# Six raw weight places and twelve input slots in the input stage of a hybrid S5 / forgetting-attention block

## The chip, the cores and the metric

One Trainium2 chip, one core. The metric is the device time of one execution in microseconds (us), the median of several runs. Engines are called PE (TensorE, matmuls and transposes), DVE (VectorE), ACT (ScalarE), POOL (GpSimd) and SP (SyncE, which here issues most transfers). Each engine runs its own instructions in order and waits on semaphores for the others.

## The reference, cut to what matters

```python
u = rms_norm(h, norm_mix)                       # x: (1, 1024, 1024) float32
proj = u @ w_in                                 # u_ssm (512), q, k, v (512 each), f (8), gates (2048)
y_ssm = gelu(s5_ssm(u_ssm, lam, dt, b, c, d))   # 32 groups, 64 complex states each, scan over 1024 tokens
glu_a, glu_b = split(y_ssm @ w_glu);  out_a = glu_a * sigmoid(glu_b)
out_b = forgetting_attention(q, k, v, f + b_forget) @ w_fox_o
h = h + (sigmoid(g_a) * out_a + sigmoid(g_b) * out_b) @ w_mix_out
m = rms_norm(mem, norm_mem_kv);  k, v = split(m @ w_mem_kv)   # 256 memory tokens, 4 heads of 128
h = h + cross_attention(rms_norm(h), k, v)
h = h + (silu(f_a) * f_b) @ w_ffn_out           # f_a, f_b = rms_norm(h) @ w_ffn_in
out = rms_norm(h)
```

Everything is float32. The change concerns the first stage (norms of `mem` and `x`, keys and values of the memory, `u_ssm`) and one step of the state-space stage.

## The kernel before, in words

**Arithmetic.** A float32 product is made of three matmuls. `split` writes a high part on ACT (a cast) and the rest on DVE, or on POOL where asked (a subtraction); `mm3` multiplies high by high, high by low and low by high.

**Stages.** `stage_in`, `stage_ssm` (32 gate products, with the state-space work of four quarters `q` among them), the attention, and a tail with mixing, cross-attention and the feed-forward part. The input stage keeps its tiles in a pool `xin`, closed before `stage_ssm` opens its own pool `qp` in the same memory.

**The input stage.** `ORDER_IN` is a list of steps written out by hand. `stage_in` walks through it and calls the function of each step's letter:

- `F` loads a tile of 128 tokens (`m`, `n` of `mem`, 0 to 7 of `x`) into an input slot; `G` loads a gain, spread over all partitions, into such a slot as well. There are 8 slots (tag `xt`).
- `Q` squares and sums on ACT, `R` makes the reciprocal root (`rsqrt`), `S` scales the tile by root and gain (`g`: on ACT and POOL), `T` transposes half a tile on PE, `E` evacuates and splits it into `mT` or `uT`.
- `D` loads a raw weight of 512 KB (0 to 3 keys, 4 to 7 values, 8 to b the state-space input from `w_in`) into a raw place, tag `raw`, of which there are 2; `W` splits it (`g`: low part on POOL). The split frees the place. The same two places serve the gate weights of the next stage.
- `K`, `V`, `U` are the products for keys, values and `u_ssm` (`U21`: quarter 2, second half of the tokens); `k`, `v`, `u` evacuate them. `k3` and `v` also store keys and values to memory. The tiles `us` that `u` fills reuse the four places of keys and values (tag `kv`), so they wait for these stores.
- `L0` issues the loads of the state-space parameters, `L1` transposes them on PE, `P` runs the next piece of their preparation on DVE.
- `X` runs warm-up matmuls on a constant at the start.

The order of emission is a priority: a scheduler at compile time merges the steps on each engine by its own estimate of what is ready, so the instructions of neighbouring steps interleave. What is once in an engine's order, or in SP's, then waits in that order.

**Roots.** `rsqrt` has two forms. With `pool`, POOL raises to the power -0.5 and DVE adds one Newton step (three instructions). Without, DVE makes a first guess from the bits and three Newton steps (ten instructions). Before, `mem` uses the first, `x` the second.

**State-space weights.** `S5.weights(q)` computes three tables for a quarter: `fb` (POOL, with scratch `w1`, `w2`), `Gm` (products of decay powers with `c` into the same scratch on POOL, subtracted on DVE), and `EC`, `ES` by doubling (POOL, the last two doublings on DVE). `turn_weights(q)` and `states(q)` use them on PE between gates 4 + 7q and 5 + 7q; `states` first loads `xg`, which `u` has stored.

Of the kernel before, what the change touches and what calls it, by code (L numbers as in the profile page):

```python
# [9 lines left out]
F32 = mybir.dt.float32  # L10
# [4 lines left out]
ALU = mybir.AluOpType  # L15
# [4 lines left out]
P = 128  # L20
D = 1024
# [17 lines left out]
RSLOT_LATE = (0, 1, 2, 3, 4, 4, 5, 5, 6, 6, 7, 7)  # L39

ORDER_IN = """
G0 Fm Qm Fn D1 X24 Qn Rm D0 Sm F1 G1 Tm0 Rn Em0 Sn Tn0 F0 Tm1 W0 Q0 Tn1 En0 F2 Q1 W1g En1 Em1 K0 D2 F3 K1 R0
S0 T00 T01 k0 E00 Q2 W2g D3 E01 D4 S1 T10 Q3 W3 k1 D5 K3 K2 W4 E10 W5 D6 R1 k2 T11 k3 S2 F4 Q4 V0 F5 S3g T30
E11 D7 Q5 F7 T20 R2 T21 E21 E20 S4 E30 W6 W7 T40 V1 D8 S5 E40 W8 T31 V2 L0 T41 E31 V3 D9 Db T50 F6 Q6 v T51 W9
E51 U00 Da Q7 L1 E41 u00 R3 S6 Wa T60 E50 S7 T61 T70 Wbg E61 U10 E60 P0 U20 u10 T71 E70 E71 u20 P1 U21 U11 U30
P2 u30 U31 u11 u31 U01 u21 P3 P4 P5 u01
"""

# [18 lines left out]
def f32(ap):  # L67
    return ap.bitcast(F32)
# [50 lines left out]
class Block:  # L119
    BANKS = {"mm": 3, "sc": 2, "pv": 2, "misc": 1}  # L120

    def __init__(self, ctx, tc):
        self.tc, self.nc = tc, tc.nc
        nc = self.nc
        self.V, self.A, self.G, self.T, self.S = nc.vector, nc.scalar, nc.gpsimd, nc.tensor, nc.sync
        self.const = ctx.enter_context(tc.tile_pool(name="const", bufs=1))
        self.small = ctx.enter_context(tc.tile_pool(name="small", bufs=3))
        self.wpool = ctx.enter_context(tc.tile_pool(name="wpool", bufs=4))
        self.dram = ctx.enter_context(tc.tile_pool(name="dram", bufs=1, space=DRAM))
        self.psum = ctx.enter_context(tc.tile_pool(name="psum", bufs=2, space=PSUM))  # L130
        self.ident = self.const.tile([P, P], F32, name="ident")
        make_identity(nc, self.ident)
        self.mhalf = self.const.tile([P, 1], F32, name="mhalf")
        nc.vector.memset(self.mhalf, -0.5)
        self.junk = self.const.tile([P, 512], BF16, name="junk")
        self.nbank = 0
# [197 lines left out]
def stage_in(B, xp, s5, x, mem, g_mix, g_kv, w_in, w_mem_kv, uT, u_d, kv_d):  # L334

    V, A, T, S, small = B.V, B.A, B.T, B.S, B.small  # L340
    junk = xp.tile([P, D], BF16, name="junk")
    mT = Act(xp, "mT", 4, 8, ML, kg=4, name="m")
    tiles, gain, ss, rs, raw, w, ps, us, kv = {}, {}, {}, {}, {}, {}, {}, [], []
    names = {"m": -2, "n": -1, **{str(t): t for t in range(NT)}}

    def xtile(name="xt"):
        return xp.tile([P, D], F32, tag="xt", bufs=8, name=name)

    def fetch(t):
        tiles[t] = xtile()  # L350
        S.dma_start(tiles[t], mem[(t + 2) * P:(t + 3) * P, :] if t < 0 else x[t * P:(t + 1) * P, :])

    def gains(i):
        gain[i] = xtile("gain")
        S.dma_start(gain[i], (g_kv if i == 0 else g_mix).partition_broadcast(P))

    def square(t):
        if t % 2 == 0:
            ss[t // 2] = small.tile([P, 2], F32, name="ss2")
        A.activation(junk, tiles[t], AF.Square, scale=1.0 / 32, accum_out=ss[t // 2][:, t % 2:t % 2 + 1])  # L360

    def root(i):
        rs[i] = B.rsqrt(ss[-1][:, i % 2:i % 2 + 1] if i < 0 else ss[i], pool=i < 0)

    def scale(t, pool):
        i = t // 2
        r = rs[t][:, 0:1] if t < 0 else rs[i][:, t % 2:t % 2 + 1]
        B.norm_scale(tiles[t], tiles[t], r, gain[0 if t < 0 else 1], pool=pool)

    def turn(t, b):  # L370
        ps[t, b] = B.turn(tiles[t], b, ("misc", "pv")[b])

    def evac(t, b):
        B.turned(ps.pop((t, b)), b, *((mT, t + 2) if t < 0 else (uT, t)))

    def wget(i):
        if i < 4:
            src = w_mem_kv[:, i * P:(i + 1) * P]
        elif i < 8:
            src = w_mem_kv[2 * (i - 4) * P:2 * (i - 3) * P, 512:1024]  # L380
        else:
            src = w_in[:, C_U + (i - 8) * P:C_U + (i - 7) * P]
        raw[i] = B.wpool.tile([P, RAW], F32, tag="raw", bufs=2, name="raw")[:, :D]
        S.dma_start(raw[i].rearrange("p (k c) -> p k c", k=D // src.shape[-1]),
                    src.rearrange("(k p) c -> p k c", p=P))

    def wsplit(i, pool):
        hl = [B.wpool.tile([P, WSLOT], F32R, tag=t_, name=t_)[:, :D] for t_ in ("whi", "wlo")]
        if i < 8:
            B.split(*hl, raw.pop(i), pool)  # L390
        else:

            B.split(*[t_.rearrange("p (k n g) -> p k n g", k=8, n=16) for t_ in hl],
                    raw.pop(i).rearrange("p (k g n) -> p k n g", k=8, g=8), pool)
        w[i] = [t_.rearrange("p (k c) -> p k c", k=2 if 4 <= i < 8 else 8) for t_ in hl]

    def keys(h):
        ps["k", h] = B.bank("mm")
        B.gemm_t(ps["k", h][:, :ML], *w[h], mT, 0, 8)

    def keys_out(h):
        if not kv:
            kv.extend(xp.tile([P, D], F32R, tag="kv", bufs=4, name="kv") for _ in range(4))
        cs = slice(h * ML, (h + 1) * ML)
        B.split(kv[0][:, cs], kv[1][:, cs], ps.pop(("k", h))[:, :ML])
        if h == 3:
            for i in range(2):
                S.dma_start(kv_d[i], f32(kv[i]))

    def values(kk):  # L410
        wh, wl = w[4 + kk]
        for t in range(2):
            if kk == 0:
                ps["v", t] = B.bank("sc")
            for k in (2 * kk, 2 * kk + 1):
                B.mm3(ps["v", t], *mT.tok(k, t), wh[:, k % 2, :], wl[:, k % 2, :], k == 0, k == 7)

    def values_out():
        for t in range(2):
            cs = slice(t * 512, (t + 1) * 512)  # L420
            B.split(kv[2][:, cs], kv[3][:, cs], ps.pop(("v", t)))
        for i in range(2, 4):
            S.dma_start(kv_d[i], f32(kv[i]))

    def ssm_in(q, h):
        ps["u", q, h] = B.bank("mm")
        B.gemm_t(ps["u", q, h], *w[8 + q], uT, h, 8)

    def ssm_out(q, h):
        if h == 0:  # L430
            us.append(xp.tile([P, D], F32, tag="kv", bufs=4, name="us"))
        uv = us[q].rearrange("p (t c) -> p t c", t=8)
        A.copy(uv[:, :, 64 * h:64 * h + 64], ps.pop(("u", q, h)).rearrange("p (c t) -> p t c", t=8))
        if h == 1:
            S.dma_start(u_d[q].rearrange("t p c -> p t c"), uv)

    prep = s5.prepare()

    acts = {"F": lambda a: fetch(names[a]), "G": lambda a: gains(int(a)), "Q": lambda a: square(names[a]),
            "R": lambda a: root(names[a]),  # L440
            "S": lambda a: scale(names[a[0]], a[1:] == "g"),
            "T": lambda a: turn(names[a[0]], int(a[1])), "E": lambda a: evac(names[a[0]], int(a[1])),
            "D": lambda a: wget(int(a, 16)), "W": lambda a: wsplit(int(a[0], 16), a[1:] == "g"),
            "K": lambda a: keys(int(a)), "k": lambda a: keys_out(int(a)), "V": lambda a: values(int(a)),
            "v": lambda a: values_out(), "U": lambda a: ssm_in(int(a[0]), int(a[1])),
            "u": lambda a: ssm_out(int(a[0]), int(a[1])), "L": lambda a: s5.load(int(a)),
            "P": lambda a: next(prep, None), "X": lambda a: B.warm(int(a))}
    for step in ORDER_IN.split():
        acts[step[0]](step[1:])
# [661 lines left out]
class S5:  # L1111
# [149 lines left out]
    def weights(self, q):  # L1261
# [5 lines left out]
        def bpow(tab, n):  # L1267
            return tab[:, :n, j4].rearrange("p k j -> p j k").unsqueeze(3).to_broadcast([P, 4, n, 16])

        def bvec(v, n):  # L1270
            return v[:, j4, :].unsqueeze(2).to_broadcast([P, 4, n, 16])
# [15 lines left out]
        Gp = Gm.rearrange("p (j two t m) -> p j two t m", two=2, t=8, m=16)  # L1287
        gv = [w.rearrange("p (j t m) -> p j t m", j=4, t=8) for w in (w1, w2)]
        for o in range(2):
            G.tensor_tensor(out=gv[0], in0=bpow(self.la[0], 8), in1=bvec(self.cT[o], 8), op=ALU.mult)  # L1290
            G.tensor_tensor(out=gv[1], in0=bpow(self.la[1], 8), in1=bvec(self.cT[1 - o], 8), op=ALU.mult)
            for two in range(2):
                h = slice(64 * two, 64 * two + 64)
                dst = Gp[64 * o:64 * o + 64, :, two]
                if o == 0:
                    V.tensor_sub(dst, gv[0][h], gv[1][h])
                else:
                    V.scalar_tensor_tensor(out=dst, in0=gv[0][h], scalar=-1.0, in1=gv[1][h],
                                           op0=ALU.mult, op1=ALU.subtract)
# [511 lines left out]
```

## Time and profile before

| | |
|---|---|
| runs | 1593.13, 1590.36, 1592.80 us; median 1592.8 |
| span of the profiled execution | 1586.7 us; the profile gives no device time of its own for it |
| what lies around the span, taken from the median | 6.1 us |
| mean granted TensorE clock | 0.988 |
| busy | PE 1534.0, DVE 1019.5, ACT 655.2, POOL 254.3 us |

The profile is one execution. A line of a timeline reads: start, length, engine, source line, operation, output<-inputs, shapes, count, and in brackets the idle time of the engine before it and what released it. In the chain of waits each line is a piece of the chain that ended last. The granted clock is a share of full speed. The lines shown in the prediction are not repeated here.

### The profile page before, as it was taken

The page shows a single profiled execution, that of the slowest core. Times are in us where ns is not written, and L with a number is a line of the kernel's source. Part 1 is how long each engine was busy: PE and PEld are TensorE (multiplying, and loading weights), DVE is VectorE, ACT ScalarE, POOL GpSimd, SP SyncE. Part 2 cuts the span into 40 slices and gives each one's busy share as a digit, 9 for nine tenths or more (in the row PEclk, how much of TensorE's full clock was granted, in tenths as well). Part 3 has the DMA queues.
Part 4 walks back from the last instruction along what each step waited for, and adds up shares of the span by engine and source line. Part 5 has one row for each costly group of instructions (what it writes and reads, how often), then busy time and mean ns, then how long its engine had stood idle before and what let it go on. Part 6 is the DMA issues. An engine that isn't in the chain of part 4 may idle for free.

```text
span 1586.7 us, 20446 instructions
## 1 busy us (share of the span) xinstructions
PE 1534.0 (97%) x7313; PEld 1261.3 (79%) x7313; DVE 1019.5 (64%) x1850; ACT 655.2 (41%) x1173; POOL 254.3 (16%) x335
## 2 busy tenths in 40 slices
PE   7799999999999899999999999999999999999997
PEld 6578888898777668888888778888888888788885
DVE  6666445344688687675555697766677776565555
ACT  6422434323576553222435564333333333254342
POOL 2027653200212124110002200100000000000001
PEclk8899999999999999999999999999999999999999
DMA  7764445652023736357412186555444554796642
GB/s 266 125 132 80 127 131 110 130 145 30 18 52 48 186 95 208 125 172 259 160 46 75 54 283 239 170 164 163 155 153 160 166 162 156 261 391 223 195 150 106
DMA packets 197940, 240.86 MB, mean 152 GB/s; under 512 B 35448, under 2 KB 126488, under 8 KB 197328
## 3 DMA queue, kind: packets, MB, share of 16 engines
q1 hardware_dynamic: 191216, 223.84, 48.2%
q10 hardware_dynamic: 6624, 15.73, 2.6%
q8 instruction: 57, 0.93, 0.2%
q14 instruction: 43, 0.35, 0.1%
HBM read 165.60 MB, written 75.86 MB: 152 GB/s over the span
## 4 chain that ended last, share of the span: by engine, by line
PE 75%; DVE 8%; DMA 7%; issue 4%; POOL 3%; ACT 2%; SPq 1%; DVEq 0%; POOLq 0%; ACTq 0%
PE mm L868 14%; PE mm L168 7%; PE pv L868 7%; PE mm L170 7%; PE mm L169 7%; PE mm L1005 4%; PE sc L868 3%; PE sc L1005 3%; PE pv L1005 3%; PE sc L168 3%; PE sc L169 3%; PE sc L170 3%; DMA raw<-in_w_in_dram 2%; PE misc L1005 1%; PE pv L168 1%
## 5 line engine op out<-in xcount | busy, mean ns | idle before, releaser
L179 DVE TENSOR_TENSOR wlo<-raw,whi 128x1024 fp32r<-128x1024 f32 (+2 forms) x121 | 132.0, 1094 | 135.1 <-ACT whi L178 133.9
L178 ACT CAST whi<-raw 128x1024 fp32r<-128x1024 f32 (+2 forms) x124 | 116.1, 940 | 220.0 <-DMA raw<-in_w_ffn_in_dram 54.1
L168 PE MATMUL mm<-uh,whi 128*128 128x512 f32 x344 | 138.8, 404 | 2.8 <-ACT whi L178 2.7
L170 PE MATMUL mm<-uh,wlo 128*128 128x512 f32 x344 | 136.5, 397 | 1.7 <-DVE wlo L179 1.7
L169 PE MATMUL mm<-ul,whi 128*128 128x512 f32 x344 | 136.4, 396 | 0.0
L179 DVE TENSOR_TENSOR ol<-or,oh 128x1024 fp32r<-128x1024 f32 x73 | 89.3, 1224 | 71.6 <-ACT oh L178 70.3
L178 ACT CAST oh<-or 128x1024 fp32r<-128x1024 f32 x73 | 76.8, 1052 | 105.3 <-PE mm L1005 33.6
L900 POOL TENSOR_TENSOR g<-a,c 128x512 f32<-128x512 f32 x22 | 35.2, 1600 | 392.8 <-ACT a L899 373.9
L170 PEld LDWEIGHTS mm<-uh,wlo 128*128 128x128 f32 x344 | 65.7, 191 | 16.5 <-DVE wlo L179 3.1
L1630 POOL TENSOR_TENSOR pl<-pf,ph 128x512 fp32r<-128x512 f32 (+1 forms) x32 | 39.7, 1239 | 241.1 <-DVE ph L1629 196.1
L168 PEld LDWEIGHTS mm<-uh,whi 128*128 128x128 f32 x344 | 65.9, 192 | 15.5 <-ACT whi L178 3.2
L169 PEld LDWEIGHTS mm<-ul,whi 128*128 128x128 f32 x344 | 66.0, 192 | 11.3
L197 POOL TENSOR_TENSOR r<-ms,mhalf 128x1 f32<-128x1 f32 x26 | 15.1, 582 | 354.9 <-DVE ms L193 344.5
L1627 ACT ACTIVATE pf<-sc 128x512 f32<-128x512 f32 (+1 forms) x96 | 46.5, 490 | 46.3 <-DVE sc L1623 28.6
L868 PE MATMUL pv<-S3h,we 128*128 128x512 f32 x176 | 58.1, 389 | 0.0
L1633 DVE TENSOR_TENSOR pl<-pf,ph 128x512 fp32r<-128x512 f32 (+2 forms) x64 | 35.1, 550 | 10.2 <-ACT ph L1632 9.5
L1005 PE MATMUL mm<-oh 128*128 128x512 f32 x106 | 41.2, 389 | 0.0
L1005 PE MATMUL mm<-ol,oh 128*128 128x512 f32 x106 | 41.2, 389 | 0.0
L1005 PE MATMUL mm<-oh,ol 128*128 128x512 f32 x106 | 41.2, 389 | 0.0
L168 PE MATMUL mm<-yh,whi 128*128 128x512 f32 x104 | 40.9, 393 | 0.0
L168 PE MATMUL sc<-uh,whi 128*128 128x512 f32 x104 | 40.8, 393 | 0.0
L170 PE MATMUL mm<-yh,wlo 128*128 128x512 f32 x104 | 40.6, 390 | 0.0
(580 smaller groups left out, 4537.5 us busy)
## 6 DMA issues: line engine op xcount, KB each, us to landing
or<-c_d SPq DMA_DIRECT2D x77, 256.0 KB
raw<-in_w_in_dram SPq DMA_DIRECT2D x22, 512.0 KB
wo<-in_w_ffn_out_dram SPq DMA_DIRECT2D x22, 512.0 KB
c_d<-g SPq DMA_DIRECT2D x44, 256.0 KB
t_d<-wo SPq DMA_DIRECT2D x44, 256.0 KB
or<-t_d SPq DMA_DIRECT2D x44, 256.0 KB
raw<-in_w_ffn_in_dram SPq DMA_DIRECT2D x20, 512.0 KB
rawb<-in_w_ffn_in_dram SPq DMA_DIRECT2D x20, 512.0 KB
```

The costliest lines, as they stand in the source:

```text
L168: T.matmul(ps, lh, rh, start=first, stop=False)
L169: T.matmul(ps, lh, rl, start=False, stop=False)
L170: T.matmul(ps, ll, rh, start=False, stop=last)
L178: self.A.copy(hi, src)
L179: (self.G if pool_lo else self.V).tensor_sub(lo, src, f32(hi))
L197: self.G.tensor_tensor(out=r, in0=v, in1=self.mhalf[:, 0:n], op=ALU.pow)
L868: T.matmul(ps, l_[:, k, :], r_, start=first and k == 0 and i == 0, stop=k == 3 and i == 2, skip_group_check=True)
L900: G.tensor_mul(g[:, 512:], a1, c1)
L1005: T.matmul(ps, l_[:, gi], r_[:, 512:], start=n < 3 and p == 0 and k == 0 or n == 7 and p == 0 and k == 0, stop=p == NP - 1 and k == 2, ski ...
L1627: self.exp = A.activation(pf[:, off:], ps[:, off:], AF.Exp)
L1630: G.tensor_sub(pl[:, off:], pf[:, off:], f32(ph[:, off:]))
L1633: V.tensor_sub(pl[:, off:], pf[:, off:], f32(ph[:, off:]))
```

## The change

- The input stage has 12 input slots instead of 8. Raw weights 2 and 5 go to a place of their own (`xraw`), 8 to b into input slots (`wr`), the others into the two `raw` places as before.
- The order of loads: weights 2 to b and tiles 2 to 7 stand earlier in the list. `L0` stands after the load of weight a, that of weight b after `L0`.
- Keys and values are stored in steps of their own: `Z0` after `Da`, `Z2` after `Db` and `U00`.
- 60 warm-up matmuls instead of 24.
- All roots of the input stage use POOL's power; the tile with the exponent has two columns for it.
- The products of decay powers with `c` run on DVE instead of POOL.
- The scratch for dynamic transfers is set to 1024 bytes.

```diff
 ORDER_IN = """
-G0 Fm Qm Fn D1 X24 Qn Rm D0 Sm F1 G1 Tm0 Rn Em0 Sn Tn0 F0 Tm1 W0 Q0 Tn1 En0 F2 Q1 W1g En1 Em1 K0 D2 F3 K1 R0
-S0 T00 T01 k0 E00 Q2 W2g D3 E01 D4 S1 T10 Q3 W3 k1 D5 K3 K2 W4 E10 W5 D6 R1 k2 T11 k3 S2 F4 Q4 V0 F5 S3g T30
-E11 D7 Q5 F7 T20 R2 T21 E21 E20 S4 E30 W6 W7 T40 V1 D8 S5 E40 W8 T31 V2 L0 T41 E31 V3 D9 Db T50 F6 Q6 v T51 W9
-E51 U00 Da Q7 L1 E41 u00 R3 S6 Wa T60 E50 S7 T61 T70 Wbg E61 U10 E60 P0 U20 u10 T71 E70 E71 u20 P1 U21 U11 U30
+G0 Fm Qm Fn D1 X60 Qn Rm D0 Sm F1 G1 Tm0 Rn Em0 Sn Tn0 F0 D2 Tm1 W0 Q0 Tn1 En0 F2 F3 D3 Q1 W1g En1 Em1 K0 F4 F5 K1 R0
+S0 T00 T01 k0 E00 Q2 W2g D4 F6 F7 D8 E01 S1 T10 Q3 W3 k1 D5 K3 K2 W4 E10 W5 D6 R1 k2 T11 k3 S2 Q4 V0 S3g T30
+E11 D7 Q5 T20 R2 T21 E21 E20 S4 E30 W6 D9 W7 T40 V1 S5 E40 T31 V2 E31 W8 T41 V3 Da Z0 L0 T50 Q6 v T51 W9
+E51 U00 Db Z2 Q7 E41 R3 S6 u00 L1 Wa T60 E50 S7 T61 T70 Wbg E61 U10 E60 T71 E70 E71 P0 U20 u10 u20 P1 U21 U11 U30
 P2 u30 U31 u11 u31 U01 u21 P3 P4 P5 u01
 """
...
-        self.mhalf = self.const.tile([P, 1], F32, name="mhalf")
+        self.mhalf = self.const.tile([P, 2], F32, name="mhalf")
...
-        return xp.tile([P, D], F32, tag="xt", bufs=8, name=name)
+        return xp.tile([P, D], F32, tag="xt", bufs=12, name=name)
...
-        rs[i] = B.rsqrt(ss[-1][:, i % 2:i % 2 + 1] if i < 0 else ss[i], pool=i < 0)
+        rs[i] = B.rsqrt(ss[-1][:, i % 2:i % 2 + 1] if i < 0 else ss[i])
...
-        raw[i] = B.wpool.tile([P, RAW], F32, tag="raw", bufs=2, name="raw")[:, :D]
+        if i > 7:
+            raw[i] = xtile("wr")
+        elif i % 3 == 2:
+            raw[i] = xp.tile([P, D], F32, tag="xraw", bufs=1, name="xraw")
+        else:
+            raw[i] = B.wpool.tile([P, RAW], F32, tag="raw", bufs=2, name="raw")[:, :D]
...
-        if h == 3:
-            for i in range(2):
-                S.dma_start(kv_d[i], f32(kv[i]))
+
+    def kv_store(i0):
+        for i in range(i0, i0 + 2):
+            S.dma_start(kv_d[i], f32(kv[i]))
...
-        for i in range(2, 4):
-            S.dma_start(kv_d[i], f32(kv[i]))
...
+            ... "Z": lambda a: kv_store(int(a)), ...
...
-            G.tensor_tensor(out=gv[0], in0=bpow(self.la[0], 8), in1=bvec(self.cT[o], 8), op=ALU.mult)
-            G.tensor_tensor(out=gv[1], in0=bpow(self.la[1], 8), in1=bvec(self.cT[1 - o], 8), op=ALU.mult)
+            V.tensor_tensor(out=gv[0], in0=bpow(self.la[0], 8), in1=bvec(self.cT[o], 8), op=ALU.mult)
+            V.tensor_tensor(out=gv[1], in0=bpow(self.la[1], 8), in1=bvec(self.cT[1 - o], 8), op=ALU.mult)
...
-    nc = _bacc.Bacc("TRN2", target_bir_lowering=False, num_devices=1)
+    nc = _bacc.Bacc("TRN2", target_bir_lowering=False, num_devices=1, dynamic_dma_scratch_size=1024)
```

More of the change, by code (lines that the diff above doesn't have):

```diff
@@ L444, in stage_in @@
             "K": lambda a: keys(int(a)), "k": lambda a: keys_out(int(a)), "V": lambda a: values(int(a)),
-            "v": lambda a: values_out(), "U": lambda a: ssm_in(int(a[0]), int(a[1])),
+            "v": lambda a: values_out(), "Z": lambda a: kv_store(int(a)), "U": lambda a: ssm_in(int(a[0]), int(a[1])),
             "u": lambda a: ssm_out(int(a[0]), int(a[1])), "L": lambda a: s5.load(int(a)),
```

## The prediction

> **What bounds the kernel now.** I read the page first.
>
> ```profile
> span 1586.7 us, 20446 instructions
> PE 1534.0 (97%) x7313; PEld 1261.3 (79%) x7313; DVE 1019.5 (64%) x1850; ACT 655.2 (41%) x1173; POOL 254.3 (16%) x335
> PE   7799999999999899999999999999999999999997
> PEclk8899999999999999999999999999999999999999
> ```
>
> TensorE (PE) is the bound of the whole kernel. Only the first slices show a PE below nine tenths and a clock below nine, and that is the input stage, the one this change rewrites. Everything after it queues behind PE, so PE time saved there should move the end one for one, unless something later comes due earlier than it can be ready. Next I cut that stage into windows at the places where PE starts, stalls and ends. Columns: stretch and length, busy time (instructions) of PE, weight load, DVE, ACT, POOL, then granted clock, DMA share, GB/s.
>
> ```profile
> core 0: us, PE busy (x) PEld busy (x) DVE busy (x) ACT busy (x) POOL busy (x), PEclk, DMA share, GB/s
> ...
> 10.40:23.20 12.80, 10.44 (x44) 9.02 (x45) 10.23 (x23) 9.67 (x16) 5.21 (x3) 0.50 0.87 308
> 23.20:48.80 25.60, 23.94 (x157) 20.89 (x157) 21.05 (x50) 14.33 (x30) 2.98 (x2) 1.00 0.74 203
> 48.80:53.80 5.00, 0.41 (x2) 0.00 (x1) 2.97 (x4) 3.00 (x6) 0.00 (x0) 1.00 0.81 111
> 53.80:65.10 11.30, 8.19 (x32) 6.68 (x33) 6.28 (x11) 4.57 (x8) 0.00 (x0) 0.81 1.02 159
> 65.10:82.00 16.90, 13.89 (x54) 10.60 (x55) 13.48 (x55) 8.25 (x12) 3.98 (x1) 0.83 0.34 83
> 82.00:112.10 30.10, 30.10 (x137) 24.95 (x136) 21.04 (x97) 7.17 (x13) 3.78 (x7) 1.00 0.62 129
> 112.10:188.00 75.90, 75.90 (x385) 64.48 (x383) 38.27 (x55) 26.08 (x40) 50.92 (x99) 1.00 0.49 102
> ```
>
> ```profile
> 1.86 4.87 PE L241 MATMUL misc<-ident 128*128 128x256 bf16 x24 [1.86 <-POOL ident masks.py:199]
> 10.40 0.48 PE L223 MATMUL pv<-ident,xt 128*128 128x128 f32 x1 [3.67 <-DVE ms L195]
> ...
> 16.96 0.80 PE L168 MATMUL mm<-mh,whi 128*128 128x256 f32 x2 [1.10 <-ACT mh L178]
> ...
> 55.34 0.78 PE L168 MATMUL mm<-uh,whi 128*128 128x512 f32 x1
> ...
> 65.10 0.31 PE L1153 MATMUL misc<-ident,prow 48*128 48x48 f32 x1 [3.08 <-issue]
> ...
> 112.12 0.39 PE L168 MATMUL sc<-uh,whi 128*128 128x512 f32 x1
> ...
> 117.56 0.39 PE L168 MATMUL mm<-uh,whi 128*128 128x512 f32 x1
> ```
>
> The first transpose runs at 10.40, the keys begin at 16.96, the first state-space product (U00) at 55.34, and the stage ends at 112.12 with the first gate. A gate, 24 matmuls like a U step, takes 117.56 - 112.12 = 5.44 us. From 10.40 to 112.1 PE idles 2.36 + 1.66 + 4.59 + 3.11 + 3.01 = 14.73 us. It also runs at half clock for all of its 10.44 us in the first window, for 3.41 us of the fourth (clock 0.81) and for about 5.8 us of the fifth (clock 0.83), which costs half of each: 5.2 + 1.7 + 2.9 = 9.8 us. So of 101.7 us about 24.5 are lost, and this is the ceiling for the input stage. From 112.1 to 188 PE is full.
>
> The chain of waits says what the idle stretches wait for (start, length, what).
>
> ```profile
> 21.39 2.40 POOL wlo L179
> 23.80 4.46 DMA raw<-in_w_mem_kv_dram
> ...
> 38.84 9.74 DMA raw<-in_w_in_dram
> ...
> 51.76 8.97 DMA raw<-in_w_in_dram
> ...
> 64.70 8.15 DMA raw<-in_w_in_dram
> ```
>
> Each late weight is issued only when one of the two raw places comes free, and then takes 8 to 10 us to land: 38.84 to 48.6, 51.76 to 60.7, 64.70 to 72.9. PE's three gaps follow them, and with each gap the clock falls. The row of 23.80 shows the same in small: the load starts when POOL's split (2.40 us) has freed its place. It is a lack of places, not of work.
>
> **The change part by part.** The profiled execution has no time of its own on the page beyond its span, 6.1 us under the median of the runs, 1592.8; I keep these 6.1 us as what lies around it, and sum from there.
>
> *Weight places and input slots.* The edit removes nothing from PE; it lets the loads be issued early. U00 needs two gains, ten input tiles and weights 0 to 8: 21 loads of 0.524 MB, 11 MB. At the 308 GB/s of the first window this is 36 us, so it has landed near 38 us, against 48.6 for weight 8 alone now. Two weights still wait: 5 for the place of weight 2, 6 and 7 for the splits of 3 and 4. The late input tile 6 no longer waits for a slot. What then remains of the 24.5 us, term by term. Opening idle: the first tiles go through the same DVE and ACT steps, 2.4 stays. The 1.7 of the third window stays. At the seam to U I take 2.0, between nothing and the 4.46 of one load from its row. In the U part, where the old idle time was 3.11 + 3.01 = 6.1, I take 2.0, between nothing and 6.1: the loads are gone as a cause, but transposes still wait for evacuations on DVE. DVE has 10.23 + 21.05 + 2.97 + 6.28 + 13.48 + 21.04 = 75 us of work in 101.7, and would have it in 87.
>
> *Warm-up of 60 instead of 24.*
>
> ```profile
> L241 PE MATMUL misc<-ident x24: 272/421/421, 1.9 to 6.5; 128*128 128x256 bf16 x24
> ...
> 6.15:9.56 3.41, 0.58 (x5) 1.00 1.10 331
> ...
> 16.39:19.80 3.41, 2.84 (x12) 0.50 0.66 202
> ...
> 30.04:33.45 3.41, 2.32 (x20) 1.00 0.80 291
> ...
> 60.76:64.17 3.41, 1.26 (x6) 1.00 0.98 184
> ```
>
> The 24 cost 4.87 / 24 = 0.203 us each; the last are shorter (272 against 421 ns), so the clock rose near 6.15. It changes in steps of 3.41 us: a window with 0.58 or 1.26 us busy is followed by half clock, one with 2.32 is not, and 2.84 busy at half clock does not lift it. Sixty last 21 x 0.203 + 39 x 0.10 = 8.2 us and end near 10.1, before the first transpose is ready at 10.40: no delay, covered by the wait for the first input tile. If the clock does not rise under them they end at 1.86 + 60 x 0.203 = 14.0, 3.6 late. After them come eight transposes and a wait until the keys; those windows would be 1.2 to 1.9 us busy, between a row that drops and one that holds. I take one window at half clock, loss 1.7 instead of 5.2, with bounds 0 and 5.2. The Trainium skill (TensorE: Matmul & The Clock Gate, Part 4: PE-mode transpose) says that transposes do not count as PE-busy in the way that matmuls do. By that rule the clock would be gone before the keys start; no row here separates the two.
>
> *Roots on POOL.*
>
> ```profile
> 7.66 0.15 DVE L195 TENSOR_SCALAR ms<-ss 128x1 f32<-128x1 f32 x1 [6.62 <-ACT junk L360]
> ...
> 8.87 0.16 DVE L203 SCALAR_TENSOR_TENSOR r<-rt,r 128x1 f32<-128x1 f32 x1
> ...
> 18.19 0.17 DVE L199 TENSOR_SCALAR r<-ms 128x2 int32<-128x2 int32 x1
> ...
> 19.96 0.16 DVE L203 SCALAR_TENSOR_TENSOR r<-rt,r 128x2 f32<-128x2 f32 x1
> ```
>
> A root with POOL's power takes 7.66 to 9.03, 1.4 us; the one of ten steps after the sum takes 18.19 to 20.12, 1.9 us. Four roots lose seven DVE steps of 0.16 each, 4.5 us of DVE work. But the power now queues behind POOL's weight splits, and DVE's own queue (evacuations and splits) stands behind the step that reads it. I put this at nothing: keys are on PE at that time. Without that cover one root costs up to 2.4 us, the length of the POOL split in the chain's first row. That lies inside the seam's bounds.
>
> *Deferred stores and SP's queue.*
>
> ```profile
> 39.27 4.72 SPq L1141 DMA_DIRECT2D craw<-in_c_re_dram  x3
> 44.04 3.58 SPq L1141 DMA_DIRECT2D craw<-in_c_im_dram  x4
> ```
>
> Both pairs of stores now stand later in SP's queue, the second behind weight b. The store of keys stands ahead of the parameter loads, the store of values ahead of the gate weights and the u stores; a wait in it holds these, which are due only a U step or more later (5.44). The seven parameter loads of these rows take 8.3 us of SP; weight a is now ahead of them, and weight b behind them is needed only for the fourth pair of U. Cost nothing; 0 to 2 us if that cover is missing. The smaller DMA scratch costs nothing: the page lists hardware and instruction queues only. The exponent tile's second column is one element of a fill at the start.
>
> *Decay products on DVE.*
>
> ```profile
> L1290 POOL TENSOR_TENSOR w<-la_re,cT_re x4: 1104/1112/1972, 119.3 to 235.5; 128x512 f32<-128x512 f32 x4
> ...
> 121.55 1.38 DVE L1296 TENSOR_TENSOR Gm<-w,w 64x512 f32<-64x512 f32 x2 [7.15 <-POOL w L1291]
> ...
> 182.75 1.16 POOL L1281 TENSOR_TENSOR fre<-w,w 128x448 f32<-128x448 f32 x1 [9.31 <-PE misc L1336]
> ...
> 189.94 2.02 PE L1361 MATMUL pv<-xg,F 128*128 128x128 f32 x16 [1.55 <-DMA xg<-u_d]
> ```
>
> Four products a quarter leave POOL (4 x 1.11 = 4.4 us) and cost DVE about 4 x 0.69 (half of the 1.38 row) = 2.8. DVE waits 7.15 us for them now, in a stretch where PE is full, so nearly all of it is off the path. The single PE stall there, 1.55 us, waits for xg, whose issue stands behind a weight split on DVE; a chain some 2 us shorter should take most of it: 1.0, between 1.55 gained and 2 lost if DVE's queue gets longer instead.
>
> *Sum.* Remaining losses 2.4 + 1.7 + 2.0 + 2.0 + 1.7 = 9.8, so 24.5 - 9.8 = 14.7, and 1.0: 15.7 us. 1592.8 - 15.7 = 1577.1, a span near 1571. With the best ends the losses are 2.4: 22.1 + 1.55 gives 1569. With the worst they are 2.4 + 1.7 + 4.46 + 6.1 + 5.2 = 19.9: 4.6 gives 1588.
>
> **Rivals.**
> Transfers are the limit, not places. Loads for U00 at the 203 GB/s of the second window take 54 us; U00 starts at 55 as now, and only the U part gains, 6.1 + 1.7 + 2.9 - 2 + 1 = 9.7: 1583. For it: a DMA share of 1.02 at 53.8 to 65.1. Against: 0.74 where the slots were short.
>
> The warm-up buys nothing: half clock until the keys have filled a window, 3.5 less: 1580.6. For it: 2.84 us busy did not lift the clock.
>
> Given back: the state-space parameters are prepared on DVE after PE's transposes at 65.10. If these stay where they are while the gates come 15 us earlier, PE waits at the first state-space output for what it gained: 1592. Against: 65.10 was itself a PE wait, and their loads in the rows above were issued by 47.6.
>
> Slower: a product on DVE must wait for POOL's last reader of the same scratch, and that one for PE (9.31 us in the row of 182.75). If the product stands in DVE's order ahead of a gate weight's split, PE runs out of gate weights. With 8 us for each of three quarters, 24 us, against 15: 1602. It decides from about 6 us each. Against it: the subtraction already waits 7.15 us there, and PE stays full.
>
> **How the numbers follow.** Forecast 0.58, transfers 0.14, warm-up 0.12, given back 0.06, slower 0.10. The time is the forecast's, 1577. From 1569 to 1588 the range holds the first three cases, 0.84 less their tails, and the worst ends of the terms. 0.2% (3.2 us) is about what a measurement can tell from no change. Faster takes the first three and a little of the fourth: 0.85; same 0.05; slower 0.10.
>
> **What would show it.** Right: w_in loads issued before 38 us, U00 near 45, the first gate near 97, no drop of the clock from 45 on, and 112.1 to 188 as full as now, only earlier. The clock step: a granted clock of 1.00 instead of 0.50 from 16.4 or 19.8 on. The DVE step: no stall for xg. Wrong: a first gate later than 107, a new PE wait on DVE's products or weight splits between gates 4 and 20, or stage lengths after the first gate longer by more than 3 us.

## The result

The changed kernel takes 1591.39 us (median of 14 runs, 1589.15 to 1596.42), the kernel before 1593.27 in the same comparison: ratio 0.9994, interval 0.9985 to 1.0003. No difference can be measured. The forecast was 1577.

The head of the page of after:

```profile
span 1590.4 us, 20482 instructions
PE 1533.6 (96%) x7349; PEld 1263.6 (79%) x7349; DVE 1026.2 (65%) x1838; ACT 655.7 (41%) x1173; POOL 240.1 (15%) x323
PE   5899999999999899999999989999999999999997
```

The first slice of PE has fallen from 7 to 5: time was lost where it should have been won. Cut at the first transpose, at U00 and at the first gate, the input stage reads so. Columns: stretch and length, busy time (instructions) of PE, weight load, DVE, ACT, POOL, granted clock, DMA share, GB/s. Before:

```profile
10.40:23.20 12.80, 10.44 (x44) 9.02 (x45) 10.23 (x23) 9.67 (x16) 5.21 (x3) 0.50 0.87 308
23.20:55.34 32.14, 25.86 (x166) 22.44 (x166) 25.48 (x57) 18.65 (x37) 2.98 (x2) 0.98 0.76 184
55.34:112.12 56.78, 50.69 (x215) 40.69 (x214) 39.33 (x158) 18.69 (x30) 7.76 (x8) 0.92 0.60 122
```

After:

```profile
10.40:23.20 12.80, 1.75 (x12) 1.28 (x12) 7.49 (x13) 7.72 (x12) 6.45 (x4) 0.68 1.07 372
23.20:58.79 35.59, 30.43 (x192) 26.89 (x193) 32.13 (x52) 24.81 (x42) 4.45 (x4) 0.92 0.77 178
58.79:114.32 55.53, 49.88 (x221) 40.30 (x219) 33.60 (x146) 14.31 (x28) 7.47 (x8) 0.94 0.47 104
```

The stage is 2.2 us longer (103.92 against 101.72): PE is busy for 4.9 us less (82.06 against 86.99), because less of its work ran at half clock, and idle for 7.1 us more (21.86 against 14.73). The first window alone idles 11.05 us, 8.7 more than before; the U part, where 6.09 were to shrink to 2.0, still idles 5.65. Behind the first gate one thing moved. From it to the first transposes of `logf`, in the attention, PE takes 355.98 - 114.32 = 241.66 us, before 355.60 - 112.12 = 243.48: the stall of 1.55 us for `xg` is gone. What follows, which the change does not touch, takes 1234.4 us in this execution and 1231.1 in that of before.

**The first loss.** PE in the timeline of after:

```profile
1.87 8.10 PE L241 MATMUL misc<-ident 128*128 128x256 bf16 x60 [1.87 <-POOL ident masks.py:199]
...
23.53 1.12 PE L223 MATMUL misc<-ident,xt 128*128 128x128 f32 x4 [9.58 <-DVE ml L179]
...
25.32 0.80 PE L168 MATMUL mm<-mh,whi 128*128 128x256 f32 x2 [0.67 <-ACT mh L178]
...
70.71 0.31 PE L1157 MATMUL misc<-ident,prow 48*128 48x48 f32 x1 [4.93 <-issue]
...
114.32 0.39 PE L168 MATMUL sc<-uh,whi 128*128 128x512 f32 x1
```

The 60 warm-up matmuls end at 9.97, in time. But the last four of the memory's transposes then wait 9.58 us for an evacuation (`ml`), and the keys start at 25.32 instead of 16.96. ACT in the same stretch, first before, then after:

```profile
13.29 0.57 ACT L178 CAST mh<-misc 128x512 fp32r<-128x512 f32 x1
```

```profile
15.63 1.06 ACT L360 ACTIVATE junk<-xt 128x1024 bf16<-128x1024 f32 x1 [1.94 <-DMA xt<-in_x_dram]
...
16.81 1.06 ACT L360 ACTIVATE junk<-xt 128x1024 bf16<-128x1024 f32 x1
...
17.86 1.03 ACT L178 CAST whi<-xraw 128x1024 fp32r<-128x1024 f32 x1
18.80 0.58 ACT L178 CAST mh<-misc 128x512 fp32r<-128x512 f32 x1
```

Before, ACT evacuates the memory at 13.29. After, the squares of the first two `x` tiles and the split of weight 2 stand ahead of it in ACT's order; ACT waits 1.94 us for the first `x` tile to land, and this first evacuation of the memory comes at 18.80. Then DVE:

```profile
18.97 0.16 DVE L201 TENSOR_TENSOR rt<-r 128x2 f32<-128x2 f32 x1 [0.81 <-POOL r L197]
19.17 2.19 DVE L202 SCALAR_TENSOR_TENSOR rt<-rt,ms 128x2 f32<-128x2 f32 x1
...
21.59 1.28 DVE L217 SCALAR_TENSOR_TENSOR xt<-xt,r,gain 128x1024 f32<-128x1024 f32 x1
22.79 0.68 DVE L179 TENSOR_TENSOR ml<-misc,mh 128x512 fp32r<-128x512 f32 x1
```

The low part of the same evacuation stands behind a root and a scaling of `x`, and one root step takes 2.19 us in place of 0.16 (why, stands in the last section). So the high part is 5.5 us later than before, and from it to the low part another 4.0 us pass.

**The second loss.** SP, then ACT and DVE, in the timeline of after:

```profile
45.88 0.80 SPq L1136 DMA_DIRECT2D prow<-in_lam_re_dram  x1
...
58.43 0.37 SPq L389 DMA_DIRECT2D wr<-in_w_in_dram  x1
```

```profile
67.97 1.91 ACT L178 CAST whi<-wr 128x1024 fp32r<-128x1024 f32 x1 [6.23 <-DMA wr<-in_w_in_dram]
69.79 0.37 ACT L178 CAST uh<-misc 128x256 fp32r<-128x256 f32 x1
...
70.19 0.42 DVE L179 TENSOR_TENSOR ul<-misc,uh 128x256 fp32r<-128x256 f32 x1 [7.25 <-ACT uh L178]
```

Weight b is asked for at 58.43, behind the parameter loads that begin at 45.88. ACT then waits 6.23 us for it, and the evacuation of a transpose (`uh<-misc`) stands behind that split. PE stops for 4.93 us before 70.71 and loses its clock (granted 0.50 from 69.6 to 76.4); the rows say "issue" there, but what comes free just before is this evacuation.

### The profile page after: what moved, and what is told of

Its sections match the earlier page's. It is cut to its first block, busy times and chain, and to the rows that moved or that the text cites. A ratio compares the mean times of both kernels' runs of the same rounds, so it can differ in the third digit from the quotient of the medians.

```text
span 1590.4 us, 20482 instructions
## 1 busy us (share of the span) xinstructions
PE 1533.6 (96%) x7349; PEld 1263.6 (79%) x7349; DVE 1026.2 (65%) x1838; ACT 655.7 (41%) x1173; POOL 240.1 (15%) x323
## 4 chain that ended last, share of the span: by engine, by line
PE 84%; DVE 5%; issue 4%; DMA 3%; ACT 2%; POOL 1%; SPq 1%; DVEq 0%; POOLq 0%; ACTq 0%
PE mm L872 15%; PE mm L168 8%; PE mm L170 8%; PE mm L169 8%; PE pv L872 7%; PE mm L1009 5%; PE sc L872 4%; PE sc L1009 4%; PE sc L168 3%; PE sc L170 3%; PE sc L169 3%; PE pv L1009 3%; PE misc L1009 2%; PE pv L168 1%; PE pv L169 1%
## 5 line engine op out<-in xcount | busy, mean ns | idle before, releaser
L179 DVE TENSOR_TENSOR wlo<-raw,whi 128x1024 fp32r<-128x1024 f32 (+2 forms) x117 | 123.3, 1056 | 130.6 <-ACT whi L178 129.5
L178 ACT CAST whi<-raw 128x1024 fp32r<-128x1024 f32 (+2 forms) x118 | 106.4, 903 | 208.4 <-DMA raw<-in_w_ffn_in_dram 54.9
L197 POOL TENSOR_TENSOR r<-ms,mhalf 128x1 f32<-128x1 f32 (+1 forms) x30 | 17.9, 599 | 371.6 <-DVE ms L193 344.0
L1104 POOL TENSOR_TENSOR sg<-sg,ga 128x512 f32<-128x512 f32 x16 | 29.6, 1874 | 72.8 <-DVE sg L1097 54.8
```

Source lines behind the costliest of these rows:

```text
L178: self.A.copy(hi, src)
L179: (self.G if pool_lo else self.V).tensor_sub(lo, src, f32(hi))
L1104: self.B.G.tensor_mul(self.out[j][:, cs], self.out[j][:, cs], ga)
```

## The experiments

Theory: the new places do what was said, but two orders eat the gain: that of ACT and DVE at the start, which came with the longer warm-up, and that of SP's queue, with weight b last. Rivals: the roots on POOL are the cause at the start; the transfers are the limit; the decay products on DVE cost what the stage wins. Times are medians; ratios are to the kernel before in the same comparison, with 95% intervals. "Keys" and "gate" are the starts of the first key product and of the first gate in the profiled execution.

| kernel | time, us | ratio | keys | gate |
|---|---|---|---|---|
| before | 1593.27 | 1 | 16.96 | 112.12 |
| after | 1591.39 | 0.9994 [0.9985, 1.0003] | 25.32 | 114.32 |
| after, warm-up 24 | 1587.48 | 0.9990 [0.9980, 1.0001] | 17.34 | 111.77 |
| after, weight b earlier | 1586.03 | 0.9970 [0.9956, 0.9983] | 25.26 | 109.91 |
| after, roots of x on DVE | 1587.30 | 0.9984 [0.9972, 0.9996] | 24.24 | 111.55 |
| warm-up 24, b earlier | 1581.35 | 0.9951 [0.9938, 0.9964] | 17.20 | 104.75 |
| before, warm-up 60 | 1601.35 | 1.0053 [1.0034, 1.0071] | 23.31 | 123.61 |
| warm-up 60, order pinned, b earlier | 1580.42 | 0.9923 [0.9903, 0.9942] | 17.08 | 105.27 |
| warm-up 24, all u weights early | 1575.37 | 0.9892 [0.9874, 0.9910] | 17.28 | 99.91 |
| the same, roots of x on DVE | 1580.05 | 0.9922 [0.9905, 0.9939] | 17.09 | 104.03 |
| warm-up 60, order pinned, all early | 1580.95 | 0.9933 [0.9922, 0.9945] | 17.15 | 105.19 |
| warm-up 24, all early, products on POOL | 1576.09 | 0.9904 [0.9890, 0.9918] | 17.09 | 99.72 |
| warm-up 60, all early | 1585.61 | 0.9959 [0.9943, 0.9975] | 25.32 | 109.24 |
| warm-up 24, order pinned, all early | 1576.09 | 0.9900 [0.9883, 0.9917] | 17.22 | 99.86 |

**1. The warm-up alone put back.** In the first line of the order:

```diff
-G0 Fm Qm Fn D1 X60
+G0 Fm Qm Fn D1 X24
...
```

> The changed kernel with 24 warm-up matmuls instead of 60, nothing else. Theory A (the number of warm-up matmuls moves the compiled order: ACT's evacuations of the memory tiles fall behind the squares of the input tiles, and PE waits 9.6 us for them from 13.9 to 23.5): that wait is gone, the keys start near 17 instead of 25.3, and U00 near 50 instead of 58.8. Theory B adds that the split of weight b, which lands at 68 and stands in ACT's queue ahead of an evacuation, still holds PE until 70.7, so the first gate comes only 1 to 4 us earlier, near 111, and the time is 1588 to 1591. Rival (the roots on POOL make the wait, since DVE stands at the step that reads them): the keys stay near 25 and the time near 1591.

The keys are back at 17.34 and the 9.58 us wait is gone, but U00 comes at 55.65 and not near 50, and the gate is only 2.5 us earlier. What was won at the start is spent in two waits of PE:

```profile
51.07 1.09 PE L223 MATMUL misc<-ident,xt 128*128 128x128 f32 x4 [3.83 <-DVE ul L179]
...
74.77 1.09 PE L223 MATMUL misc<-ident,xt 128*128 128x128 f32 x4 [7.07 <-DVE edt_p L255]
```

Ahead of the first, ACT waits 2.16 us, until 45.76, for one of the earlier u weights; run 4, with weight b in time, still has this wait. The second begins with weight b. ACT, then DVE:

```profile
67.36 1.91 ACT L178 CAST whi<-wr 128x1024 fp32r<-128x1024 f32 x1 [3.68 <-DMA wr<-in_w_in_dram]
```

```profile
69.92 2.36 DVE L250 TENSOR_SCALAR edt_k<-edt_k 128x16 f32<-128x16 f32 x1
```

Once the weight has landed, POOL's split of it (69.41 to 72.26) holds a tiny step of the parameters on DVE until 72.28, and the evacuations stand behind that step. So some 2 of the 7.07 us come on top of the wait for the transfer.

**2. Weight b alone earlier.** `Db` before `Z0 L0` in the order, in place of after `U00`:

```diff
-Da Z0 L0 T50
+Da Db Z0 L0 T50
...
-U00 Db Z2 Q7
+U00 Z2 Q7
```

> The changed kernel with the load of weight b ahead of the store of keys and the parameter loads. Theory B: the load is issued near 39 instead of 58.4, ACT no longer waits 6.2 us for it, the 4.9 us of PE at 65.8 are gone and with them the half clock from 69.6 to 76.4 (3 us): first gate near 106 instead of 114.3, time near 1584. The wait at 13.9 to 23.5 stays. Rival (the parameters themselves are what PE waits for at 65.8): the wait stays, time 1590 to 1592.

```profile
23.47 1.12 PE L223 MATMUL misc<-ident,xt 128*128 128x128 f32 x4 [9.76 <-DVE ml L179]
...
68.77 0.23 PE L1157 MATMUL misc<-ident,prow 48*128 48x48 f32 x1 [0.69 <-PE mm L170]
```

The wait at the start stays, the one before the parameters falls from 4.93 to 0.69. The gate is 4.4 us earlier, less than was expected: the U part is 6.9 us shorter (48.65 against 55.53), but U00 comes 2.5 later (61.26 against 58.79). Up to it PE is busy for 34.9 us instead of 32.2, at a lower clock (0.72 from 40 to 46, where after has 1.00).

**3. The roots of x back on DVE.**

```diff
-rs[i] = B.rsqrt(ss[-1][:, i % 2:i % 2 + 1] if i < 0 else ss[i])
+rs[i] = B.rsqrt(ss[-1][:, i % 2:i % 2 + 1] if i < 0 else ss[i], pool=i < 0)
```

> The changed kernel with the four roots of the input tiles on DVE as before. Theory A: the wait of PE before the keys stays, 8 to 10 us, since the order of ACT is the same; time 1589 to 1594. Rival (roots on POOL): the keys start near 17 and the time falls by 4 us or more.

The wait at the start stays at 8.80 us (9.58) and the keys come 1.1 us earlier: the 2.19 us root step is a small part of it, the roots on POOL are not its cause. The gate is 2.8 us earlier all the same, and the time, 1587.30, is below the 1589 to 1594 that were expected; the intervals of this run and of after overlap.

**4. Edits 1 and 2 together.**

> Both edits, 24 warm-up matmuls and weight b ahead of the parameters. Theories A and B together: keys near 17, U00 near 50, no wait at the parameter transposes, first gate 97 to 100, time 1576 to 1580, more than the two single edits add up to, because each wait hides behind the other. Rival (the transfers as a whole are the limit): the first gate not before 105, time 1584 or more.

The gate comes 9.6 us earlier than in after, where the two edits alone gave 2.5 and 4.4: each cure is hidden by the other's wait until both are made. It missed the expected gate all the same (104.75): PE still waits 3.10 us at 50.30, and ACT waits 1.54 and 0.84 us for u weights that are asked for too late.

**5. The longer warm-up in the kernel before.** The edit of 1 the other way round, in the old list.

> The kernel before with 60 warm-up matmuls instead of 24 and nothing else. Theory A: the order of ACT changes here too, three squares come ahead of the first evacuation of a memory tile; PE waits 6 to 10 us before the keys, where it waited about 2, but the waits for late weights behind it absorb part: time 1592 to 1598 against 1590. Rival (the warm-up itself is harmless and the order only matters with the rest of the change): same time as before or up to 3 us less.

```profile
20.32 1.11 PE L223 MATMUL misc<-ident,xt 128*128 128x128 f32 x4 [6.59 <-DVE ml L179]
...
23.31 0.80 PE L168 MATMUL mm<-mh,whi 128*128 128x256 f32 x2 [1.88 <-ACT mh L178]
```

One number in the list makes the old kernel 8 to 9 us slower (1601.35 against 1592.12). It was expected to cost less, and it needs none of the other edits. ACT's order has changed as in after: three squares of `x` tiles run at 15.36, 16.54 and 17.72, the evacuation at 18.77.

**6. All u weights early.** Warm-up 24; 9 and a right after 8, b before weight 7's split.

```diff
-D4 F6 F7 D8 E01
+D4 F6 F7 D8 D9 Da E01
...
-S4 E30 W6 D9 W7
+S4 E30 W6 Db W7
...
-V3 Da Z0 L0
+V3 Z0 L0
...
-U00 Db Z2 Q7
+U00 Z2 Q7
```

> 24 warm-up matmuls, and weights 9 and a loaded right after weight 8, ahead of weights 5, 6, 7, which wait for their places at the head of SP's queue; weight b ahead of the store of keys. Theory C (what is left at 44 to 50 is again ACT standing at a weight that waits in SP's queue): ACT's waits for the transfers of w_in weights go, PE's wait of 3.1 us at 47 and the half clock after it (6.8 us, cost 3.4) go, first gate near 99 instead of 104.8, time near 1576. Rival (DVE is the limit there): gate near 104, time near 1581.

This is the fastest version, 16.8 us under the kernel before (1592.12 there). SP's queue and the same three stretches, in this kernel:

```profile
19.59 10.82 SPq L389 DMA_DIRECT2D wr<-in_w_in_dram  x3
...
36.71 0.75 SPq L389 DMA_DIRECT2D wr<-in_w_in_dram  x1
```

```profile
10.40:23.20 12.80, 10.12 (x42) 8.70 (x43) 9.65 (x17) 9.26 (x15) 6.51 (x4) 0.50 1.07 371
23.20:53.08 29.88, 25.79 (x168) 22.31 (x167) 26.42 (x49) 24.28 (x43) 5.47 (x4) 1.00 0.84 224
53.08:99.91 46.83, 46.55 (x216) 37.91 (x215) 33.52 (x146) 13.38 (x25) 7.64 (x8) 1.00 0.53 115
```

All four are asked for by 37.5. From U00 to the first gate PE idles 0.28 us instead of 6.09 and runs at full clock throughout. This kernel and that of 1 differ in the loads' places in the list alone, the new places and the twelve slots are in both: the places pay only with the list in this order. Whether this order would pay without the places, no run shows.

**7. The same with the roots of x on DVE** (the edit of 3).

> The same, and the roots of the input tiles on DVE as before. If DVE's standing at POOL's power (0.7 to 0.8 us a root and the long step of 2.2 us beside POOL's split) costs more than the seven extra steps a root (4.5 us of DVE in all), the time is 1 to 3 us below e7; if DVE is the limit, it is 1 to 4 us above.

4.7 us slower, the gate 4.1 later. DVE is busy for 75.8 us of this stage instead of 69.6. So in an input stage that is short of nothing else the roots on POOL are worth 4 to 5 us; in after (3) the gate was 2.8 us later with them.

**8. The warm-up of 60 with ACT's order pinned.** The squares of tiles 0 and on, and the splits of weights 2 and on, may not be ordered before that evacuation of the memory which stands last in the list (`Em1`); weight b as in 2.

```diff
-Tm1 W0 Q0 Tn1 En0 F2 F3 D3 Q1 W1g En1 Em1 K0
+Tm1 W0 Tn1 En0 F2 F3 D3 W1g En1 Em1 Q0 Q1 K0
...
-        A.activation(junk, tiles[t], AF.Square, scale=1.0 / 32, accum_out=ss[t // 2][:, t % 2:t % 2 + 1])
+        with B.behind(B.mark if t >= 0 else None):
+            A.activation(junk, tiles[t], AF.Square, scale=1.0 / 32, accum_out=ss[t // 2][:, t % 2:t % 2 + 1])
...
-            B.split(*hl, raw.pop(i), pool)
+            with B.behind(B.mark if i > 1 else None):
+                B.split(*hl, raw.pop(i), pool)
```

> The changed kernel with all 60 warm-up matmuls and weight b ahead of the parameters, but with the squares of the input tiles and the split of weight 2 tied behind the last evacuation of the memory tiles. Theory A says that it was the order, not the PE time of the 36 added matmuls: the wait of 9.6 us before the keys is gone although 60 run, keys near 17, and the time is at or below that of the version with 24 and weight b early (1581.4), by up to 3 us for the warmer clock. Rival (60 matmuls hold the PE too long, or warm memory of the clock does not matter): keys after 20, time 1584 or more.

With the 60 matmuls in place the keys are back at 17.08, and the gate 4.6 us earlier than with the same loads and the order left free (2): at the start it is the order that costs the time, not the matmuls.

**9. Pinned order and all u weights early, with 60, and then with 24.**

> Warm-up of 60 kept, ScalarE's order pinned (the squares of the first two x tiles and the splits of weights 2 and later behind the memory's last evacuation), and weights 9 and a asked for right after weight 8, weight b ahead of the stores and parameters. If the two causes (ScalarE's order, the late asking for u weights) are all that the change lost, and add up: 11.7 us (pinned order plus weight b early against before) and 5.9 us more (the earlier asking, as with the warm-up of 24) give a first gate near 99 and a time of 1574 to 1577. If the longer warm-up also pays by the clock: first gate near 97, 1571 to 1574. If pinning leaves its own wait (4.98 us of PE at 34.35 for VectorE's root beside GpSimd's split): first gate 103 to 105, 1578 to 1581.

> The best version (warm-up of 24) with ScalarE's order pinned as in the run that kept the warm-up of 60: tells whether the 5.3 us by which that run's first gate was behind the best version's (105.2 against 99.9) come from the pinning or from the warm-up. If from the pinning (squares late, so the roots late): PE waits 3 to 5 us near 34 for VectorE's root, gate 103 to 106, time 1579 to 1581. If from the warm-up: no such wait, gate 99 to 101, time 1575 to 1577.

With 60 the early weights gave nothing more (gate 105.19), and the warm-up did not pay. With 24 the gate is at 99.86, as without the pin: pinning is harmless, the 5.3 us belong to the 60. U00 is 1.5 us later with 60 (54.55 against 53.03), the U part 3.8 longer (50.64 against 46.83). Three things in the trace of the kernel with 60. POOL and DVE:

```profile
30.37 2.35 POOL L215 TENSOR_TENSOR xt<-xt,gain 128x1024 f32<-128x1024 f32 x1 [3.75 <-ACT xt L214]
32.82 0.69 POOL L197 TENSOR_TENSOR r<-ms,mhalf 128x2 f32<-128x2 f32 x1
```

```profile
33.54 0.16 DVE L201 TENSOR_TENSOR rt<-r 128x2 f32<-128x2 f32 x1 [0.80 <-POOL r L197]
33.62 0.42 DVE L179 TENSOR_TENSOR ul<-misc,uh 128x256 fp32r<-128x256 f32 x1
```

A power waits for POOL's scaling, a root step on DVE waits for the power, and an evacuation stands behind the root step. PE waits 3.71 us for that, until 34.19. Behind the pinned steps the order of ACT and DVE still differs between the two kernels, though 60 and 24 is all that they differ in. ACT with 60, then with 24:

```profile
26.61 1.05 ACT L178 CAST whi<-raw 128x1024 fp32r<-128x1024 f32 x1 [2.00 <-DMA raw<-in_w_mem_kv_dram]
...
29.13 1.17 ACT L214 ACTIVATE xt<-xt,r 128x1024 f32<-128x1024 f32 x1
```

```profile
26.12 1.15 ACT L214 ACTIVATE xt<-xt,r 128x1024 f32<-128x1024 f32 x1 [1.69 <-DVE r L203]
...
30.42 1.06 ACT L178 CAST whi<-raw 128x1024 fp32r<-128x1024 f32 x1
```

With 60 the split of a weight that has not landed stands ahead of the scaling of `x`, and on DVE its low part (27.69) ahead of the root step that this scaling needs; with 24 the scaling comes first. POOL's scaling and the power behind it are late by this. Then PE waits 1.68 us at the parameters, at 61.95. And the clock, in two windows of this kernel:

```profile
10.40:16.60 6.20, 2.76 (x20) 1.84 (x18) 4.75 (x9) 4.57 (x8) 3.31 (x2) 1.00 1.07 372
16.60:23.20 6.60, 6.05 (x27) 5.83 (x28) 4.80 (x7) 4.60 (x9) 3.11 (x2) 0.51 1.07 372
```

It stays up while the transposes run and is at half just as the keys begin, for 6.6 us. So even with the order at the start pinned, the warm-up of 60 made the transposes of this run quicker and its keys no quicker.

**10. The warm-up of 60 alone, on the fastest version.**

> The best version with its warm-up put back to 60 and nothing else: the u weights are asked for early, so that a later start of the keys can't be hidden behind a late weight b. If the longer warm-up costs what it moves the keys by (ScalarE's order again puts squares and a weight split ahead of the memory's last evacuation): keys near 25.3, first gate 6 to 9 us later than the 99.9 of the warm-up of 24, time 1581 to 1585. If the rest of the stage absorbs it or the clock pays it back: gate within 2 us of 99.9, time 1575 to 1577.

```profile
23.53 1.11 PE L223 MATMUL misc<-ident,xt 128*128 128x128 f32 x4 [9.57 <-DVE ml L179]
```

One token apart from 6: keys at 25.32, gate 9.3 us later, some 10 us slower (ratio 0.9959 against 0.9892; in the same comparison as this one the pinned kernel with 24 took 1576.09). ACT runs squares at 15.62 and 16.80 and a split at 17.86 ahead of the evacuation at 18.79; with 24 that evacuation stands at 13.56. This is the price of the warm-up where nothing else covers it.

**11. The decay products back on POOL**, on the fastest version.

```diff
-            V.tensor_tensor(out=gv[0], in0=bpow(self.la[0], 8), in1=bvec(self.cT[o], 8), op=ALU.mult)
-            V.tensor_tensor(out=gv[1], in0=bpow(self.la[1], 8), in1=bvec(self.cT[1 - o], 8), op=ALU.mult)
+            G.tensor_tensor(out=gv[0], in0=bpow(self.la[0], 8), in1=bvec(self.cT[o], 8), op=ALU.mult)
+            G.tensor_tensor(out=gv[1], in0=bpow(self.la[1], 8), in1=bvec(self.cT[1 - o], 8), op=ALU.mult)
```

> The best version so far (warm-up of 24, u weights asked for early) with the four decay products of each quarter back on GpSimd, as in the kernel before. If moving them to VectorE is worth what the prediction put on it: 1.0 us slower than with VectorE (about 1576.5 against 1575.4), a PE wait of 1 to 2 us for xg between the first gate and gate 20. If it is worth nothing: the same time within 1 us. If the products on VectorE cost weight splits (the rival for slower): 2 us or more faster. The first gate stays at 99 to 101 by every theory.

```profile
177.59 2.02 PE L1365 MATMUL pv<-xg,F 128*128 128x128 f32 x16 [1.60 <-DMA xg<-u_d]
```

The wait for `xg` is back, 1.60 us, and it is the only one of its kind. In time the two can't be told apart (1576.09 and 1575.37, intervals overlap). The stretch itself tells more: from the first gate to the first transposes of `logf` it takes 243.52 us here and 243.48 before, and 241.61 to 241.66 in the eleven kernels with the products on DVE. These transposes, first here, then in the fastest version:

```profile
343.24 0.60 PE L1502 MATMUL misc<-ident,logf 128*8 128x128 f32 x4 [0.55 <-DVE logf L1489]
```

```profile
341.57 0.60 PE L1502 MATMUL misc<-ident,logf 128*8 128x128 f32 x4 [0.55 <-DVE logf L1489]
```

So the products on DVE are worth 1.9 us and cost nothing that shows.

## Why the prediction was wrong

**The step that failed: "no delay, covered by the wait for the first input tile".** The duration was right for after (8.10 us measured, 8.2 worked out), where the matmuls end before the first transpose. In the six other profiles with 60 they last 8.26 to 9.62 us and end as late as 11.5, up to about 1 us after the first transpose could have run, and the transposes at 13.0 to 13.3 come no later for it: as PE time the cost was indeed nothing. But the edit was costed as PE time only. It also changes the order in which the other engines' steps are laid down, and the edit as a whole costs 9.3 us at the first gate on the fastest version (10 against 6) and 11.5 in the kernel before (5). On the fastest version 4.1 of the 9.3 go with the order that was pinned (105.19 in 9, 109.24 in 10); for the other 5.3 the order behind it differs too (9), but no run separates it from the clock. That the order moves with nothing but this number is shown by four pairs of traces: before and 5, after and 1, 6 and 10, and the two of 9. Why is only argued: the order is made at compile time from an estimate of what is ready; with 36 more matmuls ahead the memory's transposes look later to it, so it puts the squares of `x` first.

**The second: weight b behind the parameter loads, "Cost nothing; 0 to 2 us".** "Needed only for the fourth pair of U" is true of PE and false of ACT. Its split stands in ACT's order ahead of the evacuation of a transpose, so a late weight stops an engine that doesn't need it yet. It cost 4.4 us at the gate by itself (2), and 4.93 us of the U part, for which 2.0 was taken, stood in one wait. Weights 9 and a were late as well: behind the loads of 6 and 7, which wait for their places in SP's queue, they were asked for at 37.88 in after. Asking for all of them early moved the gate by another 4.8 us (6 against 4). Taken one after the other from after, the early loads move the gate from 114.32 to 109.24 (10) and the warm-up of 24 from there to 99.91 (6); the forecast had 97.

**The warm-up's clock, "one window at half clock, loss 1.7 instead of 5.2".** Where the order was pinned the loss was one 3.4 us stretch (18.07 to 21.48 in run 8) or one of 6.6 us (run 9) at half clock, that is 1.7 to 3.3 us, inside the bounds. With the order left free the gain was lost before the clock could matter. The rule of the Trainium skill (TensorE: Matmul & The Clock Gate, Part 4: PE-mode transpose), that transposes do not count as PE-busy in the way that matmuls do, agrees with the two windows of run 9. These do not prove it: PE was also busy for only 2.76 of 6.20 us.

**Roots on POOL, "at nothing".** Worth 4 to 5 us with early weights (7), and a gate 2.8 us later without (3). The queueing named as their danger appeared in run 9, though behind POOL's scaling and not a weight split: 3.71 us, above the 2.4 given.

**What was right.** Loads asked for late, and not the transfers themselves: with the loads asked for early and the old warm-up the stage's losses are 2.68 + 4.09 us idle up to U00, 0.28 after it and 5.06 at half clock, 12.1 in all against 24.5, a gain of 12.4, and the gate moved by 12.2. The rival "the warm-up buys nothing" gives 14.7 - 3.5 = 11.2 for this stage. The decay products gave 1.9 for the 1.0, even more than the 1.55 named as their best (11), so "slower" by DVE's products did not happen. "Given back" gave the right time, 1592, by the wrong mechanism, so by luck: in after PE did not wait for the parameters' preparation, 82.0 to 114.3 is full. U00 "near 45" does not follow from the prediction's own terms, of which 2.6 and 3.5 us lie ahead of U00, which gives 49; the best kernel has it at 53.08. The low end of the range, 1569, leaves out the 1.7 us of the third window, which the terms say stay; with them it is 1571.

**The base.** 6.1 us were taken to lie around the span. Runs that list both times put it at 2.0 to 2.2 (for instance 1591.44 and 1589.4): the profiled execution of before was itself about 4 us quicker than its median. So 12.2 us at the gate and 1.9 behind it make 14.1 of the 16.8 us by medians. What follows the transposes of `logf`, which no edit touches, takes 1230.0 to 1234.5 us from one profiled execution to the next, so the traces can't place the rest. Left open as well: how the 5.3 us of run 9 divide between order and clock, and why the gate was earlier in run 3.

## What to carry to other kernels

Where a compiler orders the engines' queues by an estimate, no instruction is free for being covered: after an edit that adds work ahead of others, compare the order on every engine first, and cost the edit by what now stands in front of what. Of a load that moves later, ask not when its consumer on PE is due but what is queued behind its first reader. Two faults in a row hide each other: the cures gave 2.5 and 4.4 us alone and 9.6 together, so test them in pairs too.

## What was not expected of the hardware

A DVE step on 128x2 elements takes 2.19 us instead of 0.16 while POOL subtracts. POOL's row in the timeline of after:

```profile
18.97 2.38 POOL L179 TENSOR_TENSOR wlo<-xraw,whi 128x1024 fp32r<-128x1024 f32 x1
```

The step (L202) starts at 19.17 and ends at 21.36, just as that subtraction does (21.35). The Trainium skill (SBUF — State Buffer, Who interferes with whom) states that a DVE instruction with two SBUF inputs and a GpSimd instruction that reads SBUF exclude each other, the later one waiting for the whole of the other. L202 has two inputs, and the trace agrees. But a step with one input is held in the same way: L250 of run 1, 2.36 us on 128x16 elements, ended at 72.28 with the split that ended at 72.26, and in after L248, 1.59 us on 128x16, ended at 72.89 with a split that ended at 72.86. So a short DVE step beside POOL's splits is to be costed at up to the split's length, and with it whatever stands behind it on DVE.
